# The last projection of a streaming-encoder layer by Strassen's seven products

## The chip, the cores and the metric

One Trainium2 chip, of which the kernel uses one core. The metric is device time in microseconds of one launch. A launch runs five engines that each follow their own list of instructions in order: TensorE (PE in the profile, its weight loads PEld), VectorE (DVE), ScalarE (ACT), GpSimd (POOL) and SyncE (SP), which in this kernel issues nearly all transfers between memory and the on-chip buffers. They wait for each other through semaphores.

## The reference

One layer, over a sequence of 2048 positions with 1024 channels, all in float32:

```python
mod = c_act @ w_ada[l] + b_ada[l]
shift, scale, gate = jnp.split(mod[:, None, :], 3, axis=-1)
h = rms_norm(x, norm_g[l]) * (1.0 + scale) + shift
u = h @ w_in[l]
...
y_a = conformer_conv_branch(glu_in, gate_a, ...)          # ends in @ w_conv_out, 512 x 1024
...
y_b = (o * jax.nn.silu(gate_b)) @ w_sb_out[l]             # o: stick-breaking attention
y = jax.nn.sigmoid(m_a) * y_a + jax.nn.sigmoid(m_b) * y_b
x = x + gate * (y @ w_out[l])
```

The change is in the last line: `y @ w_out`, 2048 x 1024 by 1024 x 1024.

## The kernel before

Channels lie on the 128 partitions, positions along the rows. A matrix of 1024 channels by 2048 positions is cut into 8 row blocks of 128 and 4 chunks of 512 positions (`KC` = 8, `CH` = 512, `NCH` = 4, `JC` = 4). Each float32 operand of a matmul is kept as two tiles of the type fp32r: a rounded part `hi` (a cast on ACT) and a remainder `lo` (a subtraction on DVE or POOL). `mm3` then makes three matmuls per product of blocks: hi by hi, hi by lo, lo by hi. Each writes a 128 x 512 tile of PSUM, which is one bank; there are eight.

The program runs in stages: the projections out of `h`, the convolution, the attention (until about 1540 us), and the last stage, which is the one that is changed. In the last stage, each chunk `ch` goes through two steps:

- `y_tiles`: for each of 8 row blocks `j`, four blocks of `za` (the convolution branch) and four of `zb` (attention output times its gate) are multiplied with the weights `wcs[j]` into two banks, `p1` and `p2`: 8 x 3 = 24 matmuls. DVE multiplies them with the merge gates `ma` and `mb`, which were stored to memory earlier and are loaded per tile and chunk, and adds them. The sum is split into `yh` and `yl`.
- `out_tile`: for each of 8 row blocks of the output, 8 x 3 matmuls into a bank `po` (four banks take turns), then one operation on DVE that multiplies with `gate` and adds the tile of x, and a store.

`y_tiles` is a generator that yields after each three matmuls, and the first tiles of chunk 0 are issued between pieces of the attention. `p1` and `p2` have two banks each. The tiles of `ma`, `mb`, x and the loaded halves share the buffers of `io` (four). The weights w_out are split once (`resident`) and stay on chip.

All loads and stores of this stage are issued by SP, in one order, and each waits there until its buffer is free or its data are ready; what stands behind it waits too. The order on each engine comes from a scheduler that lays the instructions out at build time, within what the program's dependences allow. `high_priority` moves a piece ahead in it; `keep_in_program_order` pins it. A pool with `reuse_waits="tile"` that takes over the space of an older pool waits tile by tile.

Of the kernel before, what the change touches and what calls it, by code (L numbers as in the profile page):

```python
# [50 lines left out]
def trunk_kernel(  # L51
# [25 lines left out]
    def dram(name, shape, dt):  # L77
        return dp.tile(shape, dt, name=name, tag=name)
# [81 lines left out]
    ma_d = [[dram(f"ma{j}_{g}", [P, CH], F32) for g in range(NCH)] for j in range(KC)]  # L160
    mb_d = [[dram(f"mb{j}_{g}", [P, CH], F32) for g in range(NCH)] for j in range(KC)]
    za_d = [[dram(f"za{j}_{g}", [P, CH], F32) for g in range(NCH)] for j in range(JC)]
    o_d = [[dram(f"o{j}_{g}", [P, CH], F32) for g in range(NCH)] for j in range(JC)]

    wpa = ctx.enter_context(tc.tile_pool(name="wpa", bufs=2))
# [706 lines left out]
    with ExitStack() as s2:  # L872
# [121 lines left out]
                nc.sync.dma_start(o_d[h // 2][rc][a], oc[a])  # L994


        wcs, wo = {}, {}

        def resident(pool, src, name):
            hi = pool.tile([P, 1024], F32R, name=name + "h")  # L1000
# [2 lines left out]
            return hi, lo  # L1003

        def io(name):
            return yp.tile([P, CH], F32, tag="io", name=name, bufs=4)

        def split_z(o, t):
            nc.scalar.copy(out=t[:, 0, :], in_=o)
            nc.vector.tensor_tensor(out=t[:, 1, :], in0=o, in1=f(t[:, 0, :]), op=ALU.subtract)  # L1010

        def load_za(ch):
            z = []
            for kc in range(JC):
                t = yp.tile([P, 2, CH], F32R, tag=f"za{kc}", name=f"za{kc}")
                o = io("n")
                nc.sync.dma_start(o, za_d[kc][ch])
                split_z(o, t)
                z.append(t)
            return [t[:, 0, :] for t in z], [t[:, 1, :] for t in z]  # L1020

        def load_zb(ch):
            z = []
            for kc in range(JC):
                t = yp.tile([P, 2, CH], F32R, tag=f"zb{kc}", name=f"zb{kc}")
# [4 lines left out]
                nc.gpsimd.tensor_tensor(out=o, in0=o, in1=gb, op=ALU.mult)  # L1030
                split_z(o, t)
                z.append(t)
            return [t[:, 0, :] for t in z], [t[:, 1, :] for t in z]

        def y_tiles(ch, za, zb, psum, y):

            for j in range(KC):
# [20 lines left out]
                nc.vector.tensor_tensor(out=ma, in0=ma, in1=mb, op=ALU.add)  # L1058
                hi = yp.tile([P, CH], F32R, tag=f"yh{j}", name=f"yh{j}")
                lo = yp.tile([P, CH], F32R, tag=f"yl{j}", name=f"yl{j}")  # L1060
                nc.scalar.copy(out=hi, in_=ma)
                nc.vector.tensor_tensor(out=lo, in0=ma, in1=f(hi), op=ALU.subtract)
                y[0].append(hi)
                y[1].append(lo)
                yield

        def out_tile(ch, j, y, psum):
            ts_ = slice(ch * CH, (ch + 1) * CH)
            xt = io("xt")
            nc.sync.dma_start(xt, x_t[j][:, ts_])  # L1070
            ps = psum("po")
            dense(ps, wo[j], y, KC)
            nc.vector.scalar_tensor_tensor(out=xt, in0=ps, scalar=gate[:, j:j + 1], in1=xt,
                                           op0=ALU.mult, op1=ALU.add)
            nc.sync.dma_start(out_t[j][:, ts_], xt)


        fill = filler()
# [13 lines left out]
        prev = held = ygen = wr = yp = None  # L1092
        y = ([], [])
        psum = lambda n: pd.tile([P, CH], F32, tag="pd", name=n)

        while nf < PRE:
# [2 lines left out]
        for n_, u in enumerate(units + [None]):  # L1099
# [14 lines left out]

            def others(q, half):

                nonlocal nf, ny, ygen, wr, yp
# [5 lines left out]
                if q == LAST and not half:  # L1123
                    hst.close()
                    wr = s3.enter_context(tc.tile_pool(name="wr", reuse_waits="tile", bufs=1))
                    yp = s3.enter_context(tc.tile_pool(name="yp", reuse_waits="tile", bufs=1))
                    with tc.high_priority(offset=0):
                        za = load_za(0)
                        zb = load_zb(0)
                        wcs[1] = load_piece(wpa, w_cs[1])  # L1130
                    ygen = y_tiles(0, za, zb, lambda n: psum(n), y)
                if q >= LAST + LAG:
                    next(ygen)
# [30 lines left out]


    with s3:
        wor = s3.enter_context(tc.tile_pool(name="wor", reuse_waits="tile", bufs=1, side="right"))
        pd = s3.enter_context(tc.tile_pool(name="pd3", reuse_waits="tile", bufs=2, space=PSUM))
        psum = lambda n: pd.tile([P, CH], F32, tag=n, name=n, bufs=4 if n == "po" else 2)
        for ch in range(NCH):  # L1170
            if ch:
                y = ([], [])
# [59 lines left out]
```

## Time and profile before

| | us |
|---|---|
| median of 3 runs | 1873.2 (1872.62 to 1875.44) |
| profiled execution, its own time | 1877.81 |
| its span, first to last instruction | 1876.1 |
| PE busy | 1797.0 (96%) |
| DVE busy | 1228.2 (65%) |
| ACT busy | 812.8 (43%) |
| POOL busy | 681.3 (36%) |
| granted clock of TensorE, mean | 0.993 |
| transfers | 211.08 MB, mean 113 GB/s |

How to read it: the page of a profile gives busy time of each engine over the whole span; a row by stretch gives the same for one piece of the span, with PE, PEld, DVE, ACT and POOL in that order, then the clock that TensorE was granted, the mean busy share of the 16 DMA engines, and the rate. A group has the line of the program, the engine, the operation, what is written from what, the count, then the busy time and the mean duration of one in ns, then the idle time ahead of it with what ended it. A row of the timeline has the start, the duration, and in brackets an idle time just before it. `SPq` is the issue of a transfer on SP. Lines 115 and 120 are the helpers through which all matmuls go, so matmuls are told apart by the tiles they write: `p` for y, `po` for the last projection.

### The profile page before, as it was taken

The numbers are of one execution on the slowest core, as the hardware profiler recorded it, in microseconds if no ns is written. First come the engines' busy times: TensorE is split into PE (matmuls) and PEld (weight loads), VectorE is DVE, ScalarE is ACT, GpSimd is POOL, SyncE is SP. The second block draws the span as 40 slices with busy tenths as digits, with TensorE's granted clock in tenths as the row PEclk, the third lists the DMA queues.
The fourth block names the chain that finished last, engine by engine and source line by source line (L and its number), as shares of the span: only waits on it lengthen the run. The fifth ranks groups of instructions, "written<-read, shape, count | busy, mean of one in ns | idle before, by whom it ended". The sixth has DMA issues, their size and how long they took to land.

```text
span 1876.1 us, 27226 instructions
## 1 busy us (share of the span) xinstructions
PE 1797.0 (96%) x9612; PEld 1517.0 (81%) x9612; DVE 1228.2 (65%) x1696; ACT 812.8 (43%) x1880; POOL 681.3 (36%) x899
## 2 busy tenths in 40 slices
PE   6899999999999998999999999999999899999999
PEld 5888889899888977778877778777788677888887
DVE  7646578888879354467777777777777895334341
ACT  5465113232231122267766777776777752010110
POOL 0343111111121143466666666666666641010100
PEclk9999999999999999999999999999999999999999
DMA  8553402325132443432232323132322446353532
GB/s 288 169 186 105 137 29 80 90 67 148 45 104 93 157 141 118 149 128 81 79 96 68 102 63 109 61 93 70 99 65 88 131 143 215 107 163 96 164 95 79
DMA packets 117596, 211.08 MB, mean 113 GB/s; under 512 B 15442, under 2 KB 27730, under 8 KB 117460
## 3 DMA queue, kind: packets, MB, share of 16 engines
q1 hardware_dynamic: 116308, 207.24, 35.5%
q10 hardware_dynamic: 1152, 2.10, 0.3%
q8 instruction: 76, 1.25, 0.3%
q14 instruction: 60, 0.49, 0.1%
HBM read 137.98 MB, written 71.30 MB: 112 GB/s over the span
## 4 chain that ended last, share of the span: by engine, by line
PE 72%; DVE 8%; POOL 6%; issue 5%; DMA 5%; ACT 4%; SPq 1%; DVEq 0%; ACTq 0%; POOLq 0%
PE pd L115 38%; PE po L115 9%; PE p L115 8%; PE av L115 5%; PE pT L120 5%; PE z L115 5%; POOL w L952 3%; DVE sc L945 2%; POOL wlo L103 1%; ACT z L941 1%; DMA xt<-in_x_n_dram 1%; PE pt L120 1%; DVE tlo L979 1%; DMA wa<-in_w_ada_dram 1%; DMA gt<-ga 1%
## 5 line engine op out<-in xcount | busy, mean ns | idle before, releaser
L952 POOL TENSOR_TENSOR w<-w,sc 128x512 f32<-128x512 f32 (+1 forms) x320 | 361.6, 1130 | 251.8 <-DVE sc L945 179.1
L115 PE MATMUL pd<-hhi,whi 128*128 128x512 f32 x1024 | 413.4, 404 | 1.0 <-ACT vsg L858 1.0
L115 PE MATMUL pd<-hhi,wlo 128*128 128x512 f32 x1024 | 402.7, 393 | 0.0
L115 PE MATMUL pd<-hlo,whi 128*128 128x512 f32 x1024 | 402.5, 393 | 0.0
L945 DVE TENSOR_TENSOR_SCAN sc<-z,sc,w 128x512 f32<-128x512 f32 x192 | 245.0, 1280 | 90.9 <-ACT z L941 83.6
L103 POOL TENSOR_TENSOR wlo<-wl,whi 128x512 fp32r<-128x512 f32 x88 | 131.3, 1503 | 401.4 <-ACT whi L102 401.2
L115 PEld LDWEIGHTS pd<-hhi,wlo 128*128 128x128 f32 x1024 | 193.5, 189 | 42.5 <-POOL wlo L103 0.2
L940 ACT ACTIVATE w<-z 128x512 f32<-128x512 f32 (+1 forms) x320 | 172.2, 538 | 125.7 <-PE z L115 100.0
L115 PEld LDWEIGHTS pd<-hhi,whi 128*128 128x128 f32 x1024 | 195.5, 191 | 35.4 <-ACT vsg L858 1.4
L115 PEld LDWEIGHTS pd<-hlo,whi 128*128 128x128 f32 x1024 | 194.3, 190 | 34.3
L979 DVE TENSOR_TENSOR tlo<-pT,thi 128x512 fp32r<-128x512 f32 (+1 forms) x320 | 184.2, 598 | 35.8 <-ACT thi L978 32.4
L115 PE MATMUL z<-kt,q 128*128 128x512 f32 (+2 forms) x640 | 192.7, 382 | 5.0 <-DVE sc L945 3.5
L978 ACT CAST thi<-pT 128x512 fp32r<-128x512 f32 (+1 forms) x320 | 165.4, 527 | 61.3 <-PE pT L120 57.4
L120 PE MATMUL pT<-ident,w 128*128 128x128 f32 x1088 | 173.1, 275 | 9.8 <-POOL w L952 9.5
L120 PEld LDWEIGHTS pT<-ident,w 128*128 128x128 f32 x1088 | 137.5, 141 | 45.9 <-POOL w L952 14.5
L115 PE MATMUL pd<-whi,hhi 128*128 128x256 f32 x608 | 169.7, 287 | 3.6 <-ACT hhi L131 1.9
L941 ACT ACTIVATE z<-z 128x512 f32<-128x512 f32 (+1 forms) x320 | 171.7, 537 | 0.0
L115 PE MATMUL pd<-whi,hlo 128*128 128x256 f32 x608 | 167.0, 285 | 2.3 <-DVE hlo L131 1.7
L115 PE MATMUL pd<-wlo,hhi 128*128 128x256 f32 x608 | 154.0, 284 | 0.0
L949 DVE TENSOR_TENSOR_SCAN sc<-z,tri 128x512 f32<-128x512 f32 (+3 forms) x128 | 104.4, 819 | 53.9 <-ACT z L941 41.9
L115 PE MATMUL av<-tlo,vt 128*128 128x512 f32 (+1 forms) x320 | 123.2, 385 | 14.0 <-DVE tlo L979 10.9
L115 PEld LDWEIGHTS z<-kt,q 128*128 128x128 f32 x640 | 109.6, 189 | 24.1 <-DVE sc L945 5.4
(284 smaller groups left out, 3108.4 us busy)
## 6 DMA issues: line engine op xcount, KB each, us to landing
wl<-in_w_in_dram SPq DMA_DIRECT2D x64, 256.0 KB, 2.9
wa<-in_w_ada_dram SPq DMA_DIRECT2D x24, 512.0 KB, 5.1
wl<-in_w_qkv_dram SPq DMA_DIRECT2D x36, 256.0 KB, 2.7
xt<-in_x_n_dram SPq DMA_DIRECT2D x16, 512.0 KB, 5.5
vst<-st SPq DMA_DIRECT2D x64, 128.0 KB, 2.0
kt<-kst SPq DMA_DIRECT2D x32, 256.0 KB, 2.8
vt<-vst SPq DMA_DIRECT2D x32, 256.0 KB, 2.7
q<-qst SPq DMA_DIRECT2D x32, 256.0 KB, 2.8
```

Of the source, the lines that this page charges most:

```text
L103: (lo_eng or nc.gpsimd).tensor_tensor(out=lo[:, s], in0=wl, in1=f(hi[:, s]), op=ALU.subtract)
L115: i = nc.tensor.matmul(*a, **k)
L120: i = nc.tensor.transpose(*a)
L940: nc.scalar.activation(out=w[:, lo:], in_=z[:, lo:], func=AF.Sigmoid, scale=HD ** -0.5)
L941: nc.scalar.activation(out=z[:, lo:], in_=z[:, lo:], func=AF.Sigmoid, scale=-HD ** -0.5)
L945: nc.vector.tensor_tensor_scan(out=s[:, 1:], data0=z, data1=w, initial=s[:, 0:1], op0=ALU.mult, op1=ALU.bypass)
L949: nc.vector.tensor_tensor_scan(out=s[:, lo + 1:], data0=z[:, lo:], data1=tri[:, :CH - lo], initial=1.0, op0=ALU.mult, op1=ALU.max)
L952: nc.gpsimd.tensor_tensor(out=w[:, lo:], in0=w[:, lo:], in1=s[:, lo:CH], op=ALU.mult)
L978: nc.scalar.copy(out=thi[:, :n], in_=pT[:, :n])
L979: nc.vector.tensor_tensor(out=tlo[:, :n], in0=pT[:, :n], in1=f(thi[:, :n]), op=ALU.subtract)
```

## The change

Strassen's method multiplies two matrices of 2 x 2 blocks by seven products of blocks in place of eight, at the price of sums of blocks ahead and behind. Here w_out is cut into halves of rows and of columns (4 row blocks each), and y into halves of rows and pairs of chunks (0 with 1, and 2 with 3). The table `SEVEN` gives for each product its number and three lists: the blocks of w_out that are added, the blocks of y that are added (half, chunk, sign), and the output blocks that it is added into (half, chunk, sign).

- `prepare` makes the weights of the seven products: 28 items (seven products by four row blocks). For each it loads one or two 128 x 512 halves of w_out (`raw`, 48 loads of 256 KB in all), adds two on POOL (20 sums), casts on ACT, takes the remainder on POOL or DVE in turn (14 each), and stores the split tile (`wsp`, 512 KB) to memory as `ws`. It is issued beside the rest of chunk 0's `y_tiles` and those of chunk 1, two items for three steps.
- `y_tiles` now stores the sum itself (`y[ch, j]`), unsplit. `io` has eight buffers.
- `operands` loads the four weight tiles of a product (512 KB each) from `ws`, adds two tiles of y on POOL where the product needs a sum, and splits them. There are two sets of operand tiles, `z` and `o`, which the `za` and `zb` of the chunks use too; a product's operands are issued ahead of the product before it.
- `product` makes 4 x 4 x 3 matmuls and adds each `po` bank into one or two of the output tiles `acc` (12 buffers), which start as x; an output tile is stored after its last product.

```diff
-        for ch in range(NCH):
+        with tc.tile_pool(name="pp", reuse_waits="tile", bufs=1, side="right") as pp:
+            prep = prepare()
+            za, zb = load_za(1), load_zb(1)
+            steps(ygen, prep)
+            steps(y_tiles(1, za, zb, psum, y), prep)
+            for _ in prep:
+                pass
+        ya = s3.enter_context(tc.tile_pool(name="ya", reuse_waits="tile", bufs=1, side="right"))
+        for ch in (0, 2):
             if ch:
-                y = ([], [])
-                ygen = y_tiles(ch, za, zb, psum, y)
-            for _ in ygen:
-                pass
-            if ch + 1 < NCH:
-                za = load_za(ch + 1)
-                zb = load_zb(ch + 1)
-            for j in range(KC):
-                if ch == 0:
-                    wo[j] = resident(wr if j == 0 else wor, w_out[j], f"wo{j}")
-                out_tile(ch, j, y, psum)
+                za3, zb3 = load_za(3), load_zb(3)
+                steps(y_tiles(2, za, zb, psum, y))
+                steps(y_tiles(3, za3, zb3, psum, y))
+            order = list(SEVEN)
+            nxt = operands(order[0], ch)
+            for i, m in enumerate(order):
+                A, B = nxt
+                if i + 1 < len(order):
+                    nxt = operands(order[i + 1], ch)
+                elif ch == 0:
+                    za, zb = load_za(2), load_zb(2)
+                product(m, ch, A, B, psum)
...
+        SEVEN = {
+            2: (((1, 0, 1), (1, 1, 1)), ((0, 0, 1),), ((1, 0, 1), (1, 1, -1))),
+            4: (((1, 1, 1),), ((1, 0, 1), (0, 0, -1)), ((0, 0, 1), (1, 0, 1))),
...
+        }
+        LASTS = {(1, 0): 4, (1, 1): 3, (0, 0): 5, (0, 1): 5}
+        H = KC // 2
...
+        def prepare():
+            n = 0
+            for m, (wt, _, _) in SEVEN.items():
+                for j in range(H):
+                    def part(t):
+                        w = pp.tile([P, CH], F32, tag="raw", name="raw", bufs=4)
+                        nc.sync.dma_start(w, w_out[j + H * t[0]][:, t[1] * CH:(t[1] + 1) * CH])
+                        return w
+                    t = combined(wt, part, lambda: pp.tile([P, CH], F32, tag="sum", name="sum",
+                                                           bufs=2), nc.gpsimd)
+                    w = pp.tile([P, 2, CH], F32R, tag="wsp", name="wsp", bufs=3)
+                    nc.scalar.copy(out=w[:, 0, :], in_=t)
+                    (nc.vector if n % 2 else nc.gpsimd).tensor_tensor(
+                        out=w[:, 1, :], in0=t, in1=f(w[:, 0, :]), op=ALU.subtract)
+                    ws_d[m, j] = dram(f"ws{m}_{j}", [P, 2, CH], F32)
+                    nc.sync.dma_start(ws_d[m, j], f(w))
+                    n += 1
+                    yield
...
+        def operands(m, ch):
+            q = "zo"[turn[0] % 2]
+            turn[0] += 1
+            A, B = [], []
+            for j in range(H):
+                A.append(operand(q, "a", j))
+                nc.sync.dma_start(f(A[j]), ws_d[m, j])
+            for kc in range(H):
+                B.append(operand(q, "b", kc))
+                t = combined(SEVEN[m][1], lambda t: y[ch + t[1], kc + H * t[0]],
+                             lambda: yp.tile([P, CH], F32, tag="io", name="sum", bufs=8),
+                             nc.gpsimd)
+                nc.scalar.copy(out=B[kc][:, 0, :], in_=t)
+                nc.vector.tensor_tensor(out=B[kc][:, 1, :], in0=t, in1=f(B[kc][:, 0, :]),
+                                        op=ALU.subtract)
+            return A, B
...
+        def product(m, ch, A, B, psum):
+            for j in range(H):
+                ps = psum("po")
+                for kc in range(H):
+                    s = slice(kc * P, (kc + 1) * P)
+                    mm3(ps, A[j][:, 0, s], A[j][:, 1, s], B[kc][:, 0, :], B[kc][:, 1, :],
+                        kc == 0, kc == H - 1)
+                for r, c_, sign in SEVEN[m][2]:
+                    row, g = j + H * r, ch + c_
+                    ts_ = slice(g * CH, (g + 1) * CH)
+                    if (row, g) not in acc:
+                        acc[row, g] = ya.tile([P, CH], F32, tag="acc", name="acc", bufs=12)
+                        nc.sync.dma_start(acc[row, g], x_t[row][:, ts_])
+                    o = acc[row, g]
+                    nc.vector.scalar_tensor_tensor(
+                        out=o, in0=ps, scalar=(gate if sign > 0 else ngate)[:, row:row + 1],
+                        in1=o, op0=ALU.mult, op1=ALU.add)
+                    if LASTS[r, c_] == m:
+                        nc.sync.dma_start(out_t[row][:, ts_], o)
...
+        def steps(gen, prep=iter(())):
+            for n, _ in enumerate(gen):
+                if n % 3:
+                    next(prep, None)
```

Where the instructions come to stand. First SP's queue, at the loads of the merge gates of chunk 1 (`ma_1`, `mb_1`; the last number is that of the buffer). Before, they stand between loads of x and stores of the output of chunk 0:

```order
L1070 DMA xt<-in_x_t_dram 128x512
L1075 DMA out_dram<-xt 128x512
L1044 DMA ma<-ma_1_200 128x512
L1075 DMA out_dram<-xt 128x512
L1045 DMA mb<-mb_1_232 128x512
L1075 DMA out_dram<-xt 128x512
L1044 DMA ma<-ma_1_204 128x512
```

Now the gates of tile 0 of chunk 1 stand in the middle of the preparation, between raw loads of w_out and stores of `ws`:

```order
L1111 DMA ws_1_16563<-wsp 128x1024
L1102 DMA raw<-in_w_out_dram 128x512 x3
L1050 DMA ma<-ma_1_200 128x512
L1102 DMA raw<-in_w_out_dram 128x512 x2
L1111 DMA ws_2_16589<-wsp 128x1024
L1111 DMA ws_3_16603<-wsp 128x1024
L1102 DMA raw<-in_w_out_dram 128x512
L1111 DMA ws_0_16620<-wsp 128x1024
L1102 DMA raw<-in_w_out_dram 128x512 x3
L1051 DMA mb<-mb_1_232 128x512
L1102 DMA raw<-in_w_out_dram 128x512 x2
L1111 DMA ws_1_16635<-wsp 128x1024
```

Nine raw loads and three stores of 512 KB stand between the first line shown and the load of `mb_1_232`; before, two stores of output tiles stood between the load of x and that load.

Then POOL, behind the end of the attention. Before, it had only the products of the attention output with its gate left:

```order
L952 TENSOR_TENSOR w<-w,sc_7721 128x128
L954 AFFINE_SELECT w<-w 128x128
L975 MEMSET thi 128x128
L976 MEMSET tlo 128x128
L1030 TENSOR_TENSOR o<-o,gb 128x512 x12
```

Now sums of raw halves (L1091) and remainders of split weights (L1108) follow:

```order
L977 MEMSET tlo 128x128
L1036 TENSOR_TENSOR o<-o,gb 128x512 x2
L1091 TENSOR_TENSOR sum<-raw 128x512
L1108 TENSOR_TENSOR wsp<-sum,wsp 128x512
L1091 TENSOR_TENSOR sum<-raw 128x512 x2
L1108 TENSOR_TENSOR wsp<-sum,wsp 128x512
```

The remainder of an item stands on POOL ahead of the sums of the next two, and its cast on ACT lies between its sum and its remainder.

More of the change, by code (lines that the diff above doesn't have):

```diff
@@ L1005, in io @@
         def io(name):
[L1006 removed]
+            return yp.tile([P, CH], F32, tag="io", name=name, bufs=8)
         def split_z(o, t):
@@ L1010, in split_z, with operand @@
             nc.vector.tensor_tensor(out=t[:, 1, :], in0=o, in1=f(t[:, 0, :]), op=ALU.subtract)
+        def operand(q, half, i):
+            pool = yr if (q, half) == ("o", "b") else yp
+            return pool.tile([P, 2, CH], F32R, tag=f"{q}{half}{i}", name=f"{q}{half}{i}")
         def load_za(ch):
@@ L1065, in y_tiles @@
-                yield
[L1067 to L1075, printed above, removed]
+                y[ch, j] = (yr if ch % 2 else yp).tile([P, CH], F32, tag=f"y{j}", name=f"y{j}")
@@ new lines, in y_tiles, with combined @@
+                nc.vector.tensor_tensor(out=y[ch, j], in0=ma, in1=mb, op=ALU.add)
+                yield
+        SEVEN = {
[7 rows of a table added]
+        }
+        LASTS = {(1, 0): 4, (1, 1): 3, (0, 0): 5, (0, 1): 5}
+        H = KC // 2
+        def combined(terms, part, tmp, eng):
+            if len(terms) == 1:
+                return part(terms[0])
+            t = tmp()
+            (a, b) = terms
+            eng.tensor_tensor(out=t, in0=part(a), in1=part(b),
+                              op=ALU.add if b[2] > 0 else ALU.subtract)
+            return t
@@ L1130, in others @@
                         wcs[1] = load_piece(wpa, w_cs[1])
+                    ngate = yp.tile([P, KC], F32, name="ngate")
+                    nc.vector.tensor_scalar(out=ngate, in0=gate, scalar1=-1.0, scalar2=None,
+                                            op0=ALU.mult)
                     ygen = y_tiles(0, za, zb, lambda n: psum(n), y)
```

24 lines of the change are left out of this document (10 added, 14 removed), and 5 rows, old and new, of the table SEVEN.

## The prediction

> **What bounds the kernel now.** I read the page first, then the timeline of TensorE at the ends of the last stage, then busy time by stretch.
>
> ```profile
> span 1876.1 us, 27226 instructions
> PE 1797.0 (96%) x9612; PEld 1517.0 (81%) x9612; DVE 1228.2 (65%) x1696; ACT 812.8 (43%) x1880; POOL 681.3 (36%) x899
> ...
> PE pd L115 38%; PE po L115 9%; PE p L115 8%; PE av L115 5%; PE pT L120 5%; PE z L115 5%; POOL w L952 3%; DVE sc L945 2%; POOL wlo L103 1%; ACT z L941 1%; DMA xt<-in_x_n_dram 1%; PE pt L120 1%; DVE tlo L979 1%; DMA wa<-in_w_ada_dram 1%; DMA gt<-ga 1%
> ```
>
> TensorE is busy for 96% of the span, and the chain that ended last runs through it; `po`, the matmuls of the projection that is changed, holds 9% of that chain. Next, the timeline of PE (start, duration, what):
>
> ```profile
> 1544.30 0.62 PE L115 MATMUL p<-za,wc5h 128*128 128x512 f32 x2
> 1544.75 0.39 PE L115 MATMUL p<-za,wc5l 128*128 128x512 f32 x1
> 1544.98 0.39 PE L115 MATMUL p<-za,wc5h 128*128 128x512 f32 x1
> ...
> 1560.39 0.39 PE L115 MATMUL p<-zb,wc7l 128*128 128x512 f32 x1
> 1560.62 0.39 PE L115 MATMUL po<-yh,wo0h 128*128 128x512 f32 x1
> ...
> 1566.60 0.51 PE L115 MATMUL po<-yh,wo0h 128*128 128x512 f32 x1 [1.06 <-ACT yh L1061]
> 1567.41 0.50 PE L115 MATMUL po<-yl,wo0h 128*128 128x512 f32 x1 [0.30 <-DVE yl L1062]
> ...
> 1861.64 0.40 PE L115 MATMUL po<-yh,wo6l 128*128 128x512 f32 x1
> ...
> 1871.44 0.40 PE L115 MATMUL po<-yh,wo7l 128*128 128x512 f32 x1
> ```
>
> Durations overlap, so starts give the price. Three `p` matmuls take 1544.98 - 1544.30 = 0.68 us, 0.2267 each; 42 `po` matmuls lie from 1861.64 to 1871.44, 0.2333 each. So an output tile of the projection y costs 24 x 0.2267 = 5.44 us and a chunk of y 43.5 us. Chunk 0's y ends at 1560.6, and from there PE waits only 1.06 + 0.30 us, at 1566.
>
> **What the change takes away.** The 8 x 8 x 3 x 4 = 768 `po` matmuls become 2 pairs x 7 products x 4 x 4 x 3 = 672: 96 x 0.2333 = 22.4 us off the path. The two waits at 1566 also go (-1.4), since after chunk 0's y TensorE runs chunk 1's y.
>
> **What it adds on the engines.**
>
> ```profile
> L1073 DVE SCALAR_TENSOR_TENSOR xt<-po,gate,xt 128x512 f32<-128x512 f32 x32 | 23.7, 750 | 100.2 <-PE po L115 92.0 <-DMA xt<-in_x_t_dram 8.2
> L1062 DVE TENSOR_TENSOR yl<-ma,yh 128x512 fp32r<-128x512 f32 x29 | 20.1, 692 | 19.7 <-ACT yh L1061 19.6
> L1061 ACT CAST yh<-ma 128x512 fp32r<-128x512 f32 x29 | 18.0, 621 | 201.4 <-DVE ma L1058 201.4
> L1030 POOL TENSOR_TENSOR o<-o,gb 128x512 f32<-128x512 f32 x16 | 21.3, 1334 | 203.7 <-DMA gb<-gb 125.5 <-DMA o<-o 76.1 <-issue 2.1
> L103 POOL TENSOR_TENSOR wlo<-wl,whi 128x512 fp32r<-128x512 f32 x88 | 131.3, 1503 | 401.4 <-ACT whi L102 401.2
> ```
>
> A product lasts 48 x 0.2325 = 11.2 us on PE. Beside it stand at most 8 accumulations and 4 subtractions on DVE, 8 x 0.75 + 4 x 0.69 = 8.8 us; 4 casts on ACT, 2.5 us; 4 sums on POOL, 5.3 us. All fit, and both sets of operands start a product ahead, so I cost them at nothing; without that cover DVE's 8.8 us would show. `ngate` is one operation on 8 columns: nothing. The 32 casts of `yh`, 32 subtractions of `yl` and the splits of w_out go, but none was on the path.
>
> The preparation has 28 items: 20 have two raw halves, 8 have one. On POOL that is 20 sums x 1.33 + 14 remainders x 1.50 = 48 us; ACT 28 x 0.62 = 17 us, DVE 14 x 0.69 = 10 us. They have the rest of chunk 0's y and chunk 1's y for cover, 1543 to 1604, some 61 us: by engines alone it fits.
>
> **What it adds on the queue, which decides.** All transfers stand in one row on SP. In the new order the first raw load comes right behind the last store of the attention, and the loads of chunk 1's `ma` and `mb` stand between raw loads and `ws` stores: those of its tile 0 behind 10 and 13 stores, of tile 1 behind 20, of tile 2 behind 24 and 25, of tile 3 behind 26. A y tile needs its `ma` and `mb` before DVE frees its banks, and there are two banks each for `p1` and `p2`: tile j+2 can't start before tile j's gates have landed.
>
> ```profile
> 1543.31 0.45 SPq L994 DMA_DIRECT2D o<-oc  x1
> ```
> ```profile
> 1530.00:1540.00 10.00, 10.00 (x51) 8.04 (x50) 8.67 (x17) 5.09 (x10) 2.04 (x6) 1.00 0.57 178
> 1540.00:1560.00 20.00, 20.00 (x91) 16.59 (x91) 14.77 (x23) 7.41 (x13) 0.00 (x0) 1.00 0.64 194
> 1560.00:1570.00 10.00, 8.63 (x37) 6.59 (x36) 7.58 (x12) 5.60 (x10) 0.00 (x0) 1.00 0.82 249
> 30.00:40.00 10.00, 8.01 (x65) 7.57 (x64) 8.33 (x15) 5.42 (x11) 0.00 (x0) 1.00 0.97 341
> 36.00:38.00 2.00, 1.40 (x12) 1.19 (x10) 1.23 (x3) 1.58 (x4) 0.00 (x0) 1.00 1.00 393
> 692.00:694.00 2.00, 0.40 (x4) 0.40 (x4) 1.80 (x3) 0.51 (x2) 0.00 (x0) 1.00 0.59 220
> 696.00:698.00 2.00, 2.00 (x6) 1.56 (x5) 1.88 (x8) 0.45 (x1) 0.02 (x1) 0.51 0.14 54
> ```
> ```profile
> wa<-in_w_ada_dram SPq DMA_DIRECT2D x24, 512.0 KB, 5.1
> mb<-mb SPq DMA_DIRECT2D x32, 256.0 KB, 2.7
> wl<-in_w_out_dram SPq DMA_DIRECT2D x16, 256.0 KB, 3.3
> cv<-cb SPq DMA_DIRECT2D x4, 512.0 KB, 2.8
> ```
>
> The last three columns of the stretches are clock, share of DMA and GB/s. The 12 loads of chunk 1's operands move ahead of 1543.3 (they ran from 1558 to 1576), in place of loads of w_out that are gone; at 0.57 busy from 1530 to 1540 the engines have room: nothing. From 1543.3 until tile 3's `mb` has landed the queue must move 48 raw loads and 12 gate loads of 0.262 MB and 26 stores of 0.524 MB: 15.7 + 13.6 = 29.4 MB. Behind that come 1.9 us of landing (2.7 less its own 0.8), one multiply on DVE (0.69) and y tiles 5, 6 and 7, 3 x 5.44 = 16.3 us: 18.9 in all. Without a wait chunk 1's y ends at 1560.6 + 43.5 = 1604.1.
> - At 341 GB/s (30 to 40 us, DMA 97% busy): 86 us, so 1629.5, and y ends at 1648.4: +44 us.
> - At 249 GB/s (1560 to 1570, loads that wait for buffers between): 118 us, +76.
> - At 393 GB/s (the best 2 us): 75 us, +33.
>
> Which of them? Follow two two-half items with four raw buffers: sum ends, cast 0.62, remainder on POOL 1.50, SP issues the store and then the second half of the next-but-one item (0.7), which lands 3.3 us later, sum 1.33: 7.4 us for 2.10 MB, 283 GB/s. Nine such pairs take 67 us, the eight one-half items (6.3 MB at 341) 18, the 12 gate loads 9, and 3 us fill the pipe: 97 us, so 1640, and y ends at 1659: +55. That lies between the two longer rows; I take +55, with ends +33 and +76. The three store buffers don't decide: 0.62 + 1.50 + 2.8 (a 512 KB store, `cv<-cb`) over three is 1.6 us an item, under 3.7. PE then idles several times for microseconds; the rows at 692 and 696 show what follows: after 0.40 of 2 us busy the granted clock is 0.51 in the next window shown. That mostly falls into time already lost; for the last tiles I add 2.
>
> The Trainium skill (HBM Reference, Specifications) says that a core streaming alone measures about 425 GB/s. By that the 29.4 MB would take 69 us, the stall would be 27 us, and the time about 1878. No stretch of this trace reaches it (393 at best), so the sum goes by the rows.
>
> **Products.** In the first pair 24 weight tiles x 0.524, 16 loads and 16 stores of x and out and 12 loads for chunk 2 at 0.262 make 24.1 MB, to be moved in 7 x 11.2 = 78 us. At 341 GB/s they take 71 us, hidden; at 249 97 us, +19. I take +3 (nearest to the 341 row, since the loads are of 512 KB, as those of `wa` are that run there), ends 0 and +19. The second pair has its first weights and 12 loads of x ahead of it: 0.
>
> **End.** The last tile now gets two accumulations and two stores:
>
> ```profile
> 1871.87 0.75 DVE L1073 SCALAR_TENSOR_TENSOR xt<-po,gate,xt 128x512 f32<-128x512 f32 x1 [4.85 <-PE po L115]
> ```
> 0.75 more on DVE and 0.262 MB more at 341 GB/s (0.8): +1.5 us.
>
> **Sum.** 1876.1 - 22.4 - 1.4 + 1.5 = 1853.8 without a stall; + 55 + 2 + 3 = 1913.8. The profiled execution took 1877.81, 1.7 over its span, and stood 4.6 above the median of 1873.2; so 1913.8 + 1.7 - 4.6 = 1911.
>
> **Rivals.**
> 1. Forecast: the preparation holds chunk 1's y by 44 to 76 us. Chance 0.70.
> 2. The other side: the preparation hides, as the loads of w_out do today. For it: from 1540 to 1560 PE is busy 20.00 of 20 us while they run. Against it: that was 194 GB/s, with no stores. It gives 1853.8 - 2.9 = 1851. It pays as soon as the stall is under 22.3 us: then tile 3's `mb` is through by 1607.5, which is 29.4 MB in 64 us, 458 GB/s. Chance 0.07.
> 3. The queue keeps the DMA engines as full as in the best 2 us: 33 us of stall, 1853.8 + 33 - 2.9 = 1884; a stall of 24 would be a tie. Chance 0.11, of which 0.04 within 0.2%.
> 4. The products too wait for weights: 55 + 2 + 19 gives 1927, with 76 in place of 55 1948. For it: 249 GB/s is what the last stage reached where it waited. Against: 71 us against 78. Chance 0.12.
>
> **How the numbers follow.** The likeliest case gives 1911. The range goes from 1883 (case 3; the 341 GB/s end is 1853.8 + 44 - 2.9 = 1895) to 1936 (the 249 GB/s end, 1853.8 + 76 + 5 - 2.9 = 1932, with a part of case 4). Outside lie case 2, half of 3 and half of 4, about 0.2. Faster by over 0.2% (3.7 us, about what a measurement here can tell): 0.07; within 0.2%: 0.04; slower: 0.89.
>
> **What would show it.** Right: between 1563 and 1660 PE has gaps of several microseconds ended by DVE, DVE waiting for DMA `ma` and `mb`, and DMA above 0.85 busy near 300 GB/s; POOL is not full; later PE stays at 10 of 10; the `po` group holds 672 matmuls. Wrong: PE at 10 of 10 through chunk 1's y (case 2), a rate above 393 GB/s there (case 3), or waits at the start of products for `ws` loads (case 4). The Trainium skill (TensorE: Matmul & The Clock Gate, Part 1) holds that an idle window of about 3.4 us halves the clock for the next one; the rows at 692 and 696 agree, and by it each long gap costs up to 1.7 us more.

## The result, and the profile after

| | before | after |
|---|---|---|
| median, us | 1874.3 (1872.6 to 1878.2) | 1928.2 (1922.8 to 1929.7) |
| ratio, 95% interval | | 1.0279, 1.0253 to 1.0306 |
| profiled execution, us | 1877.81 | 1929.73 |

Slower by 54 us, where 38 were forecast and the range went to 1936. The page of the changed kernel:

```profile
span 1928.0 us, 27494 instructions
PE 1788.2 (93%) x9516; PEld 1509.4 (78%) x9516; DVE 1299.9 (67%) x1783; ACT 835.1 (43%) x1916; POOL 784.0 (41%) x973
...
DMA packets 134303, 263.53 MB, mean 137 GB/s; under 512 B 17298, under 2 KB 29586, under 8 KB 134164
...
ws<-wsp SPq DMA_DIRECT2D x28, 512.0 KB, 3.0
...
raw<-in_w_out_dram SPq DMA_DIRECT2D x48, 256.0 KB, 4.2
```

PE has 96 matmuls less and 8.8 us less of busy time, and yet the span is 51.9 us longer: PE waits. PE's timeline around chunk 1's y (waits in brackets) and at the seven products behind it:

```profile
1564.60 0.73 PE L115 MATMUL p<-oa,whi 128*128 128x512 f32 x2 [0.48 <-DVE ma L1062]
1572.36 1.19 PE L115 MATMUL p<-ob,whi 128*128 128x512 f32 x2 [4.70 <-DVE mb L1063]
1587.49 1.22 PE L115 MATMUL p<-oa,whi 128*128 128x512 f32 x2 [10.22 <-DVE ma L1062]
...
1632.50 1.22 PE L115 MATMUL p<-oa,wc3h 128*128 128x512 f32 x2 [14.57 <-DVE ma L1062]
1651.02 1.22 PE L115 MATMUL p<-oa,wc4h 128*128 128x512 f32 x2 [10.22 <-DVE ma L1062]
1661.03 0.74 PE L115 MATMUL p<-oa,wc5h 128*128 128x512 f32 x2 [2.37 <-DVE ma L1062]
...
1679.49 11.09 PE L115 MATMUL po<-zb,za 128*128 128x512 f32 x48
1690.41 11.07 PE L115 MATMUL po<-ob,oa 128*128 128x512 f32 x48
...
1744.98 11.07 PE L115 MATMUL po<-zb,za 128*128 128x512 f32 x48
```

Chunk 1's y takes from 1564.0, where chunk 0's last matmul ends, to 1679.5: 115.5 us for 43.5 us of work, a stall of 72. The products then stand end to end. The same by stretches (PE, PEld, DVE, ACT, POOL, clock, DMA share, GB/s):

```profile
1570.00:1580.00 10.00, 4.91 (x12) 3.58 (x12) 6.09 (x9) 4.98 (x9) 2.80 (x3) 0.67 0.80 312
1620.00:1630.00 10.00, 0.00 (x0) 0.00 (x0) 1.38 (x2) 1.85 (x3) 1.26 (x1) 0.54 0.93 311
1640.00:1650.00 10.00, 0.80 (x4) 0.33 (x2) 0.69 (x1) 1.85 (x3) 5.46 (x6) 0.74 0.79 273
1670.00:1680.00 10.00, 10.00 (x45) 8.03 (x44) 6.85 (x10) 2.12 (x4) 8.12 (x7) 1.00 1.02 396
1679.70:1756.00 76.30, 76.30 (x337) 63.01 (x336) 57.31 (x78) 19.90 (x33) 27.31 (x19) 1.00 0.89 305
```

No engine is full during the stall, and the DMA engines aren't either: they move 29.91 MB from 1551.4 to 1660.2, 275 GB/s at a mean share of 0.80, and 396 right behind it. Who waits then? SP's own waits from 1545 to 1660, and the end of the chain that ended last (start, duration, what):

```profile
SPq L1102 <- POOL sum L1091: 19.2, 10, 3.6
SPq L1111 <- POOL wsp L1108: 19.2, 13, 3.3
SPq L1111 <- DVE wsp L1108: 18.5, 13, 2.9
SPq L1102 <- DMA raw<-in_w_out_dram: 5.2, 4, 2.1
```
```profile
1634.23 1.73 POOL sum L1091
1635.99 0.63 ACT wsp L1107
1636.64 0.70 DVE wsp L1108
1637.36 0.33 SPq L1111
1637.78 4.35 DMA raw<-in_w_out_dram
...
1654.71 5.48 DMA ma<-ma
1660.29 0.70 DVE ma L1062
1661.03 18.62 PE p L115 x72
```

L1102 is a raw load, L1111 a store of prepared weights. Read downward, the chain is one turn of the preparation: sum, cast, remainder, the store leaves SP, and only then the raw load that stands behind it. At its end comes a gate load, `ma`, that had nothing to wait for but its place in that row.

Where the 51.9 us of span come from: the attention's end and chunk 0's y +3.35 (1560.6 to 1564.0); the stall of chunk 1's y +72.0; `po` 672 matmuls in 152.9 us where 768 and two waits took 180.6, -27.7; y of chunks 2 and 3 +3.5 (90.6 for 87.0); the last accumulations and stores +0.7.

### The profile page after: what moved, and what is told of

Same layout as the page of the kernel before. It is cut to its first block, busy times and chain, and to the rows that moved or that the text cites. A ratio compares the mean times of both kernels' runs of the same rounds, so it can differ in the third digit from the quotient of the medians.

```text
span 1928.0 us, 27494 instructions
## 1 busy us (share of the span) xinstructions
PE 1788.2 (93%) x9516; PEld 1509.4 (78%) x9516; DVE 1299.9 (67%) x1783; ACT 835.1 (43%) x1916; POOL 784.0 (41%) x973
## 4 chain that ended last, share of the span: by engine, by line
PE 67%; DMA 8%; DVE 8%; POOL 7%; issue 5%; ACT 4%; SPq 1%; DVEq 0%; POOLq 0%; ACTq 0%
PE pd L115 39%; PE po L115 7%; PE p L115 5%; PE av L115 5%; PE z L115 5%; PE pT L120 5%; POOL w L953 3%; DMA raw<-in_w_out_dram 2%; DVE sc L946 2%; DMA gt<-ga 1%; POOL sum L1091 1%; DMA gb<-gb 1%; ACT z L942 1%; DMA wl<-in_w_qkv_dram 1%; DVE tlo L980 1%
## 5 line engine op out<-in xcount | busy, mean ns | idle before, releaser
L120 PEld LDWEIGHTS pT<-ident,w 128*128 128x128 f32 x1088 | 137.5, 141 | 45.2 <-POOL w L953 14.1
L115 PE MATMUL av<-tlo,vt 128*128 128x512 f32 (+1 forms) x320 | 123.2, 385 | 16.3 <-DVE tlo L980 13.0
```

What stands on the lines that cost most here:

```text
L115: i = nc.tensor.matmul(*a, **k)
L120: i = nc.tensor.transpose(*a)
```

## The experiments

The theory to begin with: the loss is chunk 1's y alone, whose gate loads stand in SP's one row behind a preparation that crawls by its chain of buffers. Rivals: the rate of the DMA engines is the limit; the products cost too; the lowered clock costs.

| kernel | median, us | ratio to before, 95% | chunk 1's y ends | waits of PE in the products |
|---|---|---|---|---|
| changed kernel | 1928.2 | 1.0253 to 1.0306 | 1679.5 | 0 |
| e1, one product's weights | 1857.1 | 0.9897 to 0.9937 | 1614.6 | 0 |
| e2, four buffers, sums in place | 1926.1 | 1.0247 to 1.0302 | 1673.4 | 0 |
| e3, seven buffers, sums in place | 1924.6 | 1.0251 to 1.0283 | 1676.0 | 0 |
| e4, gates ahead | 1933.4 | 1.0295 to 1.0341 | 1607.6 | 76.1 |
| e5, e3 with stores on ACT | 1909.0 | 1.0148 to 1.0198 | 1632.7 | 22.4 |
| e6, each half loaded once | 1903.7 | 1.0131 to 1.0168 | 1654.6 | 0 |
| e7, e6 with stores on ACT | 1885.2 | 1.0038 to 1.0073 | 1605.7 | 23.5 |
| e8, e7 with gates ahead | 1890.4 | 1.0054 to 1.0101 | 1607.1 | 30.8 |
| e9, e7 with remainders on DVE | 1879.9 | 1.0023 to 1.0050 | 1607.4 | 20.0 |
| e10, e9 with items earlier | 1880.4 | 1.0020 to 1.0039 | 1607.0 | 20.2 |
| e11, e9 with half of the sums on DVE | 1877.7 | 1.0009 to 1.0030 | 1603.1 | 19.2 |
| e12, e11 with 20 of 28 items | 1873.3 | 0.9981 to 1.0004 | 1604.6 | 11.7 |

The last two columns are the profiled execution's: the start of the first `po` less its wait, and the sum of the waits in PE's timeline. Each ratio is to executions of the kernel before in the same set, whose median went from 1874.1 to 1875.9; so times of different sets differ by a microsecond or two for no reason of the kernel's.

**e1: the products without their preparation.**

```diff
-            for m, (wt, _, _) in SEVEN.items():
+            for m, (wt, _, _) in list(SEVEN.items())[:1]:
...
-                nc.sync.dma_start(f(A[j]), ws_d[m, j])
+                nc.sync.dma_start(f(A[j]), ws_d[2, j])
```

> Only the four weight tiles of product 2 are prepared (4 of 28 items), and all seven products use them; the other six products' weights are left out. Bytes, matmuls and every other step of the products stay. Theory 1 (the loss is chunk 1's y held behind the preparation; the products give their whole gain): the 72 us of stall go, but for the 4 to 8 us by which four items delay the first gates, so 1928 - 72 + 0 to 8 = 1856 to 1864, about 10 us under the kernel before, and PE without a wait above 3 us from 1565 on. Rival 2 (the products themselves cost: their loads, their sums on POOL, their accumulations on DVE): the stall shrinks, but waits appear in the products, and the time stays above 1874. Rival 3 (a part of the loss is the clock after PE's gaps): the y tiles of chunk 1 keep lasting over 5.44 us even without gaps; above 1864.

1857.1, the only kernel here that is clearly under the kernel before; but it leaves out the weights of six products, so it only shows where the time goes. PE's timeline has one wait from 1540 to 1700:

```profile
1570.98 0.71 PE L115 MATMUL p<-ob,whi 128*128 128x512 f32 x2 [2.86 <-DVE mb L1063]
...
1614.60 11.07 PE L115 MATMUL po<-zb,za 128*128 128x512 f32 x48
```

So the products with all their loads, sums and accumulations bring no wait, and the 24 items that are left out are worth 71 us, as much as the stall: the preparation is what makes the kernel slower. The second rival falls. The third can't be judged by this run, since the gaps and the low clock go together. The chain that ended last can: followed back over the whole stall, it holds no matmul from 1551 to 1661, so slow matmuls cost time only in the last tiles, 18.62 us for 72, where 0.2333 us each would make 16.8.

**e2 and e3: is it the buffers?** The sum goes over its first half; four raw buffers, and then seven.

```diff
-                    t = combined(wt, part, lambda: pp.tile([P, CH], F32, tag="sum", ...
+                    ab = [part(t) for t in wt]
+                    t = ab[0]
+                    if len(ab) > 1:
+                        nc.gpsimd.tensor_tensor(out=t, in0=ab[0], in1=ab[1], op=...)
-                        w = pp.tile([P, CH], F32, tag="raw", name="raw", bufs=4)
+                        w = pp.tile([P, CH], F32, tag="raw", name="raw", bufs=7)   # e3 only
```

> The sum of two raw halves is written over the first of them (no sum buffers), still four raw buffers. So a raw buffer stays taken through cast and remainder, 2 us longer per item. Theory 1 (the preparation crawls by its chain of buffers): slower than 1928 by 10 to 30 us (20 items, at most 2.1 us each, half of them hidden): 1938 to 1958, DMA in the stretch 1560 to 1650 under 270 GB/s. Rival (the rate of the DMA engines bounds it): same bytes, so 1925 to 1932.

> As the kernel with sums in place, but seven raw buffers (the space of the sum buffers and the slack). Same bytes, same instructions as that one. Theory 1: more loads in flight, so the 29.4 MB go at 340 GB/s instead of 270, 22 us sooner: about 1906 (at 390 GB/s 1895), and 30 us or more under the four-buffer form. Rival (rate of the DMA engines): 1925 to 1932 as the four-buffer form. A third outcome, within 5 us of 1928 but with the four-buffer form well above: then three store buffers or POOL's order of work hold it, not the raw buffers.

1926.1 and 1924.6, not 20 us up and not 22 down: the theory's buffer chain falls, and so far the rival of the DMA rate stands. But SP's waits in e3 from 1545 to 1660 say where the time went:

```profile
SPq L1114 <- POOL wsp L1111: 43.7, 14, 5.2
SPq L1114 <- DVE wsp L1111: 18.9, 12, 3.9
```

With seven buffers no raw load waits for its buffer any more, and the same time is spent at the stores: 62.6 us, for the same row's turn. A free buffer is of no use to a load that stands behind a store whose data aren't ready. That is the theory from here on (1b): one row, in order, with waiting stores in it.

**e4: gates ahead.**

```diff
                 if n % 3:
-                    next(prep, None)
+                    with tc.high_priority(offset=-LATE):
+                        next(prep, None)
```

> The preparation gets the later place in the order: the loads of chunk 1's ma and mb stand ahead of most raw loads and stores on SP; the same work otherwise. Theory 1: chunk 1's y loses its stall (ends near 1610 instead of 1679), but the preparation has as many bytes and the same chain left, and its rest now stands ahead of the loads of x, out and weights for the first products, so PE waits there instead: the first products wait until the preparation ends near 1650 to 1660, the stall is 35 to 60 us instead of 72: 1890 to 1915. Rival (only the place of the gates matters, the rest hides beside the products): 1856 to 1866. Rival (DMA rate is the bound): the waits only move, 1920 to 1930.

The negative offset gives the preparation a later place, so the gates come ahead of it. Chunk 1's y now runs through (first product at 1607.6), but the time is 1933.4, 18 us above what the theory gave. One wait has the whole stall:

```profile
1607.63 11.08 PE L115 MATMUL po<-zb,za 128*128 128x512 f32 x48
1694.76 13.28 PE L115 MATMUL po<-ob,oa 128*128 128x512 f32 x48 [76.05 <-DVE acc L1151]
```
```profile
1685.65 2.92 SPq L1111 DMA_DIRECT2D ws<-wsp  x2
1688.62 7.75 SPq L1149 DMA_DIRECT2D acc<-in_x_t_dram  x12
```

The tiles of x (`acc`, the pool `ya`) lie in the space of the preparation's buffers, and their loads leave right behind the last store of `ws`. The first product fills the four `po` banks, and the second can't start until they are accumulated. The theory had the place of the new wait right, but not its length: it put the preparation's end at 1650 to 1660, and the last stores left at 1688. So the place of the gates alone is not the cause: whatever stands first, the preparation's end is waited for. The number lies nearest to the rival of the DMA rate (1920 to 1930, the waits only move); e5 decides between them.

**e5: the stores leave the row.** On e3, one word:

```diff
-                    nc.sync.dma_start(ws_d[m, j], f(w))
+                    nc.scalar.dma_start(ws_d[m, j], f(w))
```

> As the kernel with sums in place and seven raw buffers, whose trace shows SP waiting 62.6 us at the 26 stores (for the remainders of POOL and DVE) and at no raw load; now the 28 stores are issued from ACT's queue, the raw loads and gate loads stay on SP. Same bytes and operations. Theory 1b (the one row is the brake: a store that waits for its item's arithmetic holds the raw loads behind it, however many buffers are free): the loads run ahead, the 29.4 MB go at 340 to 390 GB/s, chunk 1's y ends 20 to 35 us sooner: 1890 to 1905. Rival A (DMA rate with stores and loads mixed is the bound): 1920 to 1928. Rival B (the arithmetic chain sum, cast, remainder on POOL and ACT is the bound): 1915 to 1925 with POOL over 60% busy in the stretch.

1909.0, 15.5 us under e3 with the same bytes, buffers and arithmetic: 4 us outside the range of theory 1b, but y ends 43 us sooner (1632.7), and 22.4 us of wait come back in the products, two of the four here:

```profile
1636.15 4.58 PE L115 MATMUL po<-zb,za 128*128 128x512 f32 x12 [3.49 <-DMA za<-ws]
...
1670.85 12.71 PE L115 MATMUL po<-ob,oa 128*128 128x512 f32 x48 [14.12 <-issue]
```

From 1552 to 1650 32.06 MB moved at 327 GB/s, where e3 has 29.92 MB at 272 from 1548 to 1658. So the rate of e3 was not the engines' limit, and POOL is 51% busy from 1550 to 1650 where rival B asked for over 60. Theory 1b holds for the stall of y; a part of the stall moved to the products. The Trainium skill (DMA: Bandwidth & Descriptors, Issuing engines are not separate DMA queues) says that transfers started from several engines interleave on the same 16 DMA engines, and that this saves only the time to start them. No run here speaks against the first half. For the second the measurement decides: starting a store takes 0.33 us here, 9 us for 28, and what was saved is the waiting of the loads behind them.

**e6: each half loaded once.** Rows outside, products inside, six raw buffers, stores on SP.

```diff
-            for m, (wt, _, _) in SEVEN.items():
-                for j in range(H):
+            for j in range(H):
+                half = {}
+                for m, (wt, _, _) in SEVEN.items():
                     def part(t):
-                        w = pp.tile([P, CH], F32, tag="raw", name="raw", bufs=4)
+                        if t[:2] not in half:
+                            w = pp.tile([P, CH], F32, tag="raw", name="raw", bufs=6)
...
```

> Loop over the four rows outside, over the seven products inside: each half of w_out is loaded once (16 raw loads instead of 48, 8.4 MB less), six raw buffers; stores stay on SP. 21 MB are left ahead of tile 3's gates. Theory 1b (loads behind waiting stores): the 32 loads that go are those that waited, so an item costs about its POOL time, 48 us of POOL in all and 60 to 70 us until the gates: 1880 to 1895. Rival A (DMA rate, 277 GB/s as measured): 76 us instead of 109: 1895. Rival B (POOL, ACT arithmetic is the bound): no gain, 1915 to 1925.

1903.7, 24.5 less, with 8.4 MB less; y ends at 1654.6. The gain is 9 to 24 us short of the first theory's: the rate fell to 254 GB/s (23.12 MB from 1549 to 1640), since SP still waits 59.5 us at the stores. 8.4 MB at 275 GB/s are 31 us, so fewer bytes did help, but in this row they didn't go faster.

**e7 and e8: both, then the gates ahead as well.** The two edits above together; e8 adds e4's.

> As that, with the stores on ACT's queue: chunk 1's gates stand behind 16 raw loads alone. Theory 1b: chunk 1's y loses nearly all of its stall; the preparation ends near 1615 to 1630, limited by POOL, so the first product waits 5 to 25 us for its last weights: 1858 to 1885. Rival A (DMA rate): 21 MB at 277 GB/s end at 1627, some 20 us of wait at the products: 1875 to 1885. Rival B (arithmetic chain): the preparation still ends near 1650 and the products wait 45 us: 1895 to 1910.

> As that, with the preparation placed later in the order than chunk 1's y. Theory 1b: as the kernel before in this set or up to 10 us better or worse, the stall only changes its place: 1855 to 1885. Rival (the place in the order still decides): more than 10 us apart from it.

e7 took 1885.2, at the upper end of what 1b gives. e8 took 1890.4, 5 us outside its range and 5 from e7: the later place helps no more here than in e4. Stretches of e7:

```profile
1570.00:1580.00 10.00, 10.00 (x44) 8.06 (x43) 8.73 (x9) 2.33 (x5) 7.08 (x5) 1.00 1.04 380
1630.00:1640.00 10.00, 0.00 (x0) 0.00 (x0) 9.61 (x7) 3.02 (x6) 9.29 (x7) 0.50 0.74 257
```
```profile
1622.42 4.64 PE L115 MATMUL po<-zb,za 128*128 128x512 f32 x12 [8.38 <-DMA za<-ws]
1642.20 13.11 PE L115 MATMUL po<-ob,oa 128*128 128x512 f32 x48 [15.14 <-issue]
```

Put beside the same stretch of the changed kernel (PE 4.91, 312 GB/s): PE is full, the DMA engines are full, and chunk 1's y has no wait at all. Time and waits of e7 would also fit rival A (1875 to 1885, some 20 us at the products), but not its rate: from 1550 to 1600 the engines move 369 GB/s at a share of 0.99, where rival A took 277. What is left are 23.5 us at the first two products. POOL and DVE are both over 90% busy at the end.

The label `issue` hides what the longer of the two waits is. DVE's accumulations of the first product, and SP:

```profile
1639.26 0.74 DVE L1154 SCALAR_TENSOR_TENSOR acc<-po,gate,acc 128x512 f32<-128x512 f32 x1
1641.35 0.75 DVE L1154 SCALAR_TENSOR_TENSOR acc<-po,ngate,acc 128x512 f32<-128x512 f32 x1 [1.35 <-issue]
```
```profile
SPq L1152 <- DMA ws<-wsp: 8.9, 1, 8.9
```

The second product starts 0.10 us behind the second accumulation, which empties the first bank. The load of its x tile left SP at 1638.1, after SP had waited 8.9 us at the loads of x (L1152) for a store of `ws` to land. So it is e4's wait for the bank again. In e5 and e8 to e11 the second product also starts 0.10 or 0.11 us behind the second accumulation; in e5 and e11 that one or the one before it had waited for its x tile too, in e8 to e10 DVE comes to it without a pause, from a last remainder or from splitting operands.

**e9, e10 and e11: arithmetic off POOL.** All remainders on DVE; then an item after every step of y; or (from e9) every second sum on DVE.

```diff
-                    (nc.vector if n % 2 else nc.gpsimd).tensor_tensor(
+                    nc.vector.tensor_tensor(                                        # e9
...
-                if n % 3:
-                    next(prep, None)
+                next(prep, None)                                                    # e10
...
-                                                           bufs=1), nc.gpsimd)
+                                                           bufs=1), nc.vector if n % 2 else nc.gpsimd)   # e11
```

> As the kernel with loop over rows outside and the stores on ACT's queue, whose chunk 1's y no longer waits, while POOL is 93 to 99% busy from 1600 to 1640 and PE waits 8.4 and 15.1 us for the first products' weights. All 28 remainders now on DVE (14 of them were on POOL, 14 x 1.38 = 19 us). Theory 1c (with the queue freed, POOL's work is the bound of the preparation): the last weights come 12 to 19 us sooner, the two waits shrink from 23.5 to 5 to 12 us: 1866 to 1874, a tie with the kernel before or just under. Rival A (DMA rate): 1880 to 1886, as that kernel. Rival C (DVE becomes the bound, as its operations lengthen to 0.9 to 1.3 us beside POOL's): 1880 to 1890.

> As that, and an item of the preparation is put into the order after every step of y, not after two of three, so its work stands a third ahead. Theory 1c: the POOL sums of w_out no longer stand behind the sums of y for the first products; another 3 to 8 us: 1860 to 1870, faster than the kernel before. Rival (the items come as fast as loads and POOL allow, order or no): within 3 us of that one.

> As the one with all remainders on DVE, and ten of the 20 sums of halves on DVE too (10 x 1.4 = 14 us off POOL, 10 x 0.7 to 1.2 on to DVE, which then has some 60 of the 60 us from 1550 to 1610 less what it needs for y, 20 us). Theory 1c: the preparation ends near 1610, PE waits under 5 us: 1858 to 1868. Rival C (DVE as the bound): 1870 to 1885, with DVE over 90% busy from 1560 to 1620.

1879.9, 1880.4, 1877.7: each misses its main number. 19 us taken off POOL shorten the waits by 3.5 us only; the earlier place does nothing (the rival was right); another 14 us give 0.8. So POOL was busy but not the limit that theory 1c made of it. Rival C stays open: its ranges hold 1877.7 and all but hold 1879.9, but in e11 DVE is 82% busy from 1560 to 1620, where it asked for over 90. Stretches of e11:

```profile
1550.00:1560.00 10.00, 10.00 (x46) 8.24 (x45) 6.84 (x10) 2.97 (x5) 2.04 (x2) 1.00 1.04 395
1580.00:1590.00 10.00, 10.00 (x44) 8.03 (x43) 6.59 (x11) 2.08 (x4) 2.91 (x2) 1.00 1.00 389
```

POOL at 2 to 3 of 10, the DMA engines at their full share: from 1550 to 1622 they move 25.98 MB at 361 GB/s. As in e7 up to 1600, the DMA engines are near their limit, now for all of the preparation but its end.

**e12: fewer bytes.** The eight items of one half are not prepared, but loaded in the product ahead of their own and split there.

```diff
-                for m, (wt, _, _) in SEVEN.items():
+                for m, (wt, _, _) in ((k, v) for k, v in SEVEN.items() if len(v[0]) > 1):
...
-                nc.sync.dma_start(f(A[j]), ws_d[m, j])
+                if len(SEVEN[m][0]) > 1:
+                    nc.sync.dma_start(f(A[j]), ws_d[m, j])
+                else:
+                    (r, c_, _), = SEVEN[m][0]
+                    o = io("wo")
+                    nc.sync.dma_start(o, w_out[j + H * r][:, c_ * CH:(c_ + 1) * CH])
+                    nc.scalar.copy(out=A[j][:, 0, :], in_=o)
+                    nc.gpsimd.tensor_tensor(out=A[j][:, 1, :], in0=o, in1=f(A[j][:, 0, :]), op=ALU.subtract)
```

> As the kernel with half of the sums on DVE (chunk 1's y without a wait, DMA at 340 to 395 GB/s from 1550 to 1630, 19.2 us of wait in the first two products), but the eight items that have one half (products 4 and 3) are no longer prepared: those weights are loaded as they are and split beside the product ahead of their own (cast on ACT, remainder on POOL). 8 stores of 0.524 MB less before the products (4.2 MB, 11 us at 370 GB/s), product 4's weights need no store, 8 casts and 8 remainders less there. Theory 1d (with the queue freed, bytes at the best DMA rate and the last item's chain are what is left): 8 to 16 us less than that kernel: 1862 to 1870, faster than the kernel before (ratio 0.993 to 0.998). Rival (what is left is the chain from the last raw load to the first accumulation, not the bytes): within 4 us of that kernel, 1874 to 1880. Rival (the splits beside the products hold POOL): waits over 2 us inside later products, above 1876.

1873.3, ratio 0.9981 to 1.0004: between the two expectations, and no difference from the kernel before that can be measured. In the profiled execution (1868.6, the lowest of its twelve) one long wait is left, beside 1.8 us in the second seven products:

```profile
1625.62 13.23 PE L115 MATMUL po<-ob,oa 128*128 128x512 f32 x48 [9.91 <-DVE acc L1162]
```
```profile
1622.41 1.75 DVE L1142 TENSOR_TENSOR zb<-sum,zb 128x512 fp32r<-128x512 f32 x1
1624.07 0.74 DVE L1162 SCALAR_TENSOR_TENSOR acc<-po,gate,acc 128x512 f32<-128x512 f32 x1
```
```profile
SPq L1160 <- DMA ws<-wsp: 8.9, 1, 8.9
```

It is the wait for the bank again, and two things end it nearly together. The load of the second x tile left SP at 1620.2, after 8.9 us of waiting for a store of `ws`, and took 3.1 us to land, so it was there at about 1623.3. DVE came to the first accumulation at 1624.07, without a pause from splitting operands. So it isn't shown that either alone would have taken the wait away. What the longer executions of this kernel (up to 1879.3) lose isn't shown, as none of them has a trace. A separate place for the first tiles of x, or accumulations ahead of the splits on DVE, was not tried.

## Why the prediction was right, and where its sizes were off

- **The direction and the mechanism.** Right: gaps of several microseconds from 1564 to 1661 that DVE's `ma` and `mb` end, gates that land late, POOL not full, PE at 10 of 10 in the products. e1 shows by itself that the preparation is the loss.
- **-22.4 and -1.4.** They measured -27.7, 3.9 more than forecast. The term went by the old spacing of 0.2333 us; in the products 48 matmuls start 10.92 us after the 48 before (1679.49, 1690.41), 0.2275 each. Nothing in the prediction expected that; why the spacing changed isn't shown.
- **Everything beside the products at nothing, and +3 for their loads.** Nothing was right for both: PE is busy 76.30 of 76.30 us, at 305 GB/s. The end, put at +1.5, measured +0.7.
- **The stall, +55 and 2 for the clock.** It measured 72, and this is the term that was mis-sized, within its ends (33 and 76). Step by step: the first raw load left at 1551.4, not 1543.3 (+8.1). 3.35 of it is the attention's later end. The rest is a load of chunk 0's gates (L1051) that stands between the attention's last store (1548.2) and the first raw load, and that waited for its `io` buffer. The chain shows who held it, an operand of chunk 1:

```profile
1543.94 5.09 DMA gb<-gb
1549.20 1.82 POOL o L1036
1551.04 0.32 SPq L1051
```

These operand loads were put at nothing. I read the start off the order and asked what stands ahead of it, but not whether that waits. From the first raw load to the last gate's landing took 108.8 us, not 98.9 (+9.9): the turn was costed with a landing of 3.3 us, and beside the stores the median is 4.2; by nine pairs that is an estimated 8 us. The last tiles took 18.62 for 16.3 + 2. Together: 57 + (8.1 - 3.35) + 9.9 + 0.3 = 72.
- **The reason given for the rate.** The turn was followed through the right steps (sum, cast, remainder, store, next load) but put down to "four raw buffers". e2 and e3 show that their number is without effect, and e5 that the store ahead of the load is what holds it.
- **The rivals.** The preparation that hides came near with four edits (e11) and to a tie with five (e12). Its point of decision, a stall of 22.3 us, was put too high: 19.2 to 20.2 us of wait still measure 1.0020 to 1.0037, 11.7 a tie. (e11's waits are those of an execution of 1874.7 us, 3 under its median.) The losses not foreseen (below), and the slow matmuls after a wait (13.11 us for a product in e7, not 11.07), which stand against the larger gain of the products, lie between; not all of it is accounted for. The rate of the best 2 us, 393, was within reach of the engines but not of this row. The Trainium skill's figure for a core streaming alone (HBM Reference, Specifications: about 425 GB/s) would have made the stall an estimated 27 us. Here 396 in 10 us was the most that the changed kernel reached, and 361 over 72 us what a freed preparation did.
- **Not foreseen:** +3.35 at the attention's end and +3.5 in the y of chunks 2 and 3. Up to 1560, PE waits 8.0 us for DVE's `sc` where it waited 3.5 before; why isn't shown. Of the 3.5, 1.9 is one wait for a gate load, and 1.3 the spacing of chunk 2's matmuls: from the operand tiles `oa` and `ob` they start 0.2333 us apart, from `za` and `zb` in chunk 3 0.2267, again for no reason that is shown. Chunk 1's y reads `oa` and `ob` too, so 1.3 of the 72 are of this kind.
- **The sum.** Stall +15.0, products -3.9, their loads -3, the end -0.8, not foreseen +3.3 and +3.5: 14.1 of the 14.2 us between 1913.8 and the span of 1928.0. So 22 us of loss and 8 of gain were missing, and that they cancel in part is luck.
- **The clock.** The wait of 14.57 us is followed by pairs of matmuls of 1.22 us in place of 0.63, and the 12 matmuls from 1632.50 to 1637.78 take 5.28 us, where 0.2333 each would make 2.8. The Trainium skill (TensorE: Matmul & The Clock Gate, Part 1) has half the clock after an idle window of about 3.4 us. The pairs agree; but 2.5 us for a long gap is more than the 1.7 that the prediction worked out from that page. Ahead of the last gap it cost nothing, as the gates decide when a tile may start: the chain holds no matmul from 1551 to 1661.

## What to carry to other kernels

When work is moved onto a queue that issues in order, ask of each entry not how long it takes but what it waits for: a store that waits for arithmetic holds every load behind it, and neither free buffers nor free DMA engines show that. Give waiting stores another queue than the loads that others need, before buffers, order or arithmetic are tuned: here that gave 15.5 us alone and 18.5 on top of fewer loads, while more buffers and the other order gave nothing. And when a stall moves without shrinking (e4), look for what is freed only at the end, here the space that the next stage's tiles share. A wait that the profile gives no reason for (`issue`) can be read from what ended 0.1 us ahead of it.

## What the runs showed of the hardware that was not expected

DVE's operations aren't of fixed length. In e7 from 1545 to 1680 (busy us and mean ns behind the bar), where POOL has much to do:

```profile
L1065 DVE TENSOR_TENSOR y<-ma,mb 128x512 f32<-128x512 f32 x12 | 14.2, 1182 | 0.3
...
L1063 DVE TENSOR_TENSOR mb<-p,mb 128x512 f32<-128x512 f32 x12 | 8.2, 680 | 2.0 <-PE p L115 2.0
```

The sum with both sources on chip in SBUF (`ma`, `mb`) takes 1182 ns, where the product that reads a PSUM bank (`p`) takes 680; in the kernel before, where POOL is busy for 15.7 of the 310 us from 1560 to 1870, the two took 691 and 691. The prediction used 0.69 us for such operations. The Trainium skill (SBUF — State Buffer, Who interferes with whom) has it that a DVE instruction with two inputs in SBUF contends with a GpSimd instruction that reads SBUF, and one with at most one such input does not. The rows agree. It may also be why work moved from POOL to DVE in e9 and e11 bought little, but no run here shows that.
